# Stick-breaking attention: weights formed transposed in PSUM, queries and values over the full array

## The chip, the cores and the metric

The kernel runs on one core of one Trainium2 chip. The metric is the device time of one execution in microseconds (us); three runs of the kernel before gave 3334.37, 3337.85 and 3341.75, median 3337.85.

## What is computed

One decoder layer over 1024 tokens of width 1024, in float32. The part that matters here is the stick-breaking attention, 8 heads of width 64, computed for blocks of 128 tokens:

```python
z = jnp.einsum('bhtd,bhsd->bhts', q[:, :, t0:kl], k[:, :, :kl]).astype(jnp.float32) * scale
causal = s_idx < t_idx
log_beta = jax.nn.log_sigmoid(z)
log_one_minus = jnp.where(causal, jax.nn.log_sigmoid(-z), 0.0)
tail = lax.cumsum(log_one_minus, axis=3, reverse=True) - log_one_minus
w = jnp.where(causal, jnp.exp(log_beta + tail), 0.0)
outs.append(jnp.einsum('bhts,bhsd->bhtd', w.astype(v.dtype), v[:, :, :kl]))
```

Since log_sigmoid(z) = z - softplus(z) and log_sigmoid(-z) = -softplus(z), the weight is exp(z - R), where R is the sum of softplus(z) over the position itself and all later causal ones: a running sum taken from the right. Beside attention the layer has an mLSTM branch (4 heads), gates and projections, two layer norms, and PEER, which picks 128 of 16384 experts per token and sums their rows.

## The kernel before

**Blocks.** The tokens are cut into 8 token blocks of 128 and these into three groups (`BLOCKS`, line 66) of 2, 3 and 3, called block 0, 1 and 2 here. `main` (line 1141) takes each group through layer norm and projection, then attention merged with the mLSTM branch and the gates (line 1148), then the merge of branches, the keys and the choice of experts. Expert rows of five token blocks are gathered one by one: GpSimd issues an indirect DMA for a row of each of 128 tokens (line 1079) into one of K = 6 `vr` buffers, and VectorE multiplies and sums it (through `Chain`, line 139). These rows are sprinkled between the steps of the main chain by the times that the steps `yield`. The other three token blocks go through all 16384 experts as dense products at the end (`dense`, line 1009).

**Attention** (line 552) works through rows and chunks. A row is one head `e` of a pair `pr` and one token block `j`; it has `nb` key blocks, 1 to 8, and is cut into chunks of at most four: one chunk up to four key blocks, two beyond that. Blocks 0, 1 and 2 have 16, 24 and 24 rows, 16, 32 and 48 chunks, and 24, 96 and 168 key blocks. A chunk passes four steps, in a software pipeline (line 628) in which round k runs `s1(k)`, `s2(k-1)`, `s3(k-2)` and `s4(k-3)`:

- `s1` (line 575): TensorE multiplies the 64 rows of the head's queries with the keys (line 583, stationary operand 64 x 128) into a `z` bank and adds the causal mask (line 585). ScalarE forms softplus in `asp` (Abs, Exp, Ln) and its other part in `art` (Relu); three of the four passes scale by 0.125 or run in place.
- `s2` (line 594): VectorE takes the running sum from the right (line 597), carried from the row's first chunk to its second, and forms z * 0.125 minus it in `art` (line 599), reading z from PSUM; ScalarE takes the Exp.
- `s3` (line 602): TensorE transposes the weights, 128 columns at a time, into an `m` bank (line 607), and ScalarE copies them out to `awT` (line 609).
- `s4` (line 612): if all chunks of the row stand in `row["done"]`, TensorE multiplies values and weights (line 622, stationary operand 128 x 64) into an `m` bank, and ScalarE copies the 64 rows to `osT` (line 625).

**Order and buffers.** The code is traced and then scheduled: each engine's queue is in the order in which a planner's model finds instructions ready, with the code's order as priority, and each engine runs its queue strictly in that order. Tiles come from rings: `z` and `m` banks of PSUM, two each (line 181), `c2` tiles of 512 columns, seven (`NC2`, line 37), used by attention and by most other steps. A reader that is late keeps a slot, and what needs the slot waits. The descriptors of the indirect DMAs use a scratch of 8192 bytes per partition of SBUF (line 1228).

```python
        for k in range(N + 3):
            if k < N:
                s1(k)
            if 0 <= k - 1 < N:
                s2(k - 1)
            if 0 <= k - 2 < N:
                s3(k - 2)
            if 0 <= k - 3 < N:
                s4(k - 3)
```

Of the kernel before, what the change touches and what calls it, by code (L numbers as in the profile page):

```python
# [10 lines left out]
F32 = mybir.dt.float32  # L11
# [3 lines left out]
AF = mybir.ActivationFunctionType  # L15
OP = mybir.AluOpType
# [4 lines left out]
P = 128  # L21
# [12 lines left out]
ORDER = [(0, 1), (2, 3, 4)]  # L34
NC4 = 4
NR4 = 2
NC2 = 7
NCS = 7
RANKS = [(0, 0, 1, 16), (16, 1, 2, 8), (24, 2, 3, 5), (29, 3, 4, 4), (33, 4, 5, 3), (36, 5, 8, 2), (42, 8, 16, 1)]
NC50 = 50  # L40
# [79 lines left out]
def body(ctx: ExitStack, tc: tile.TileContext, a, out):  # L120
    nc = tc.nc
# [3 lines left out]
    vec, pe, pool, dma = nc.vector, nc.tensor, nc.gpsimd, nc.sync  # L125
# [49 lines left out]
    act = Act()  # L175

    def T(shape, dt, tag, bufs=1):
        return sb.tile(shape, dt, name=tag, tag=tag, bufs=bufs)

    def PT(tag, shape=(P, 512)):  # L180
        return ps.tile(list(shape), F32, name=tag, tag=tag, bufs={"g": 4, "z": 2, "m": 2}[tag])

    def c6(name, shape=(P, 4, W), dt=F32):
        return sb.tile(list(shape), dt, name=name, tag="c6", bufs=8)

    def c4(name, shape=(P, D)):
        return sb.tile(list(shape), F32, name=name, tag="c4", bufs=NC4)
# [4 lines left out]
    def c2(name, shape=(P, 512), dt=F32):  # L192
        return sb.tile(list(shape), dt, name=name, tag="c2", bufs=NC2)

# [3 lines left out]
    first = [c4("xt") for _ in BLOCKS[0]]  # L198
# [4 lines left out]
    ident = T([P, P], F32, "ident")  # L203
    make_identity(nc, ident)
    identr = T([P, P], F32R, "identr")
    vec.tensor_copy(identr, ident)
    alf = T([P, P], F32, "alf")
    vec.tensor_scalar(alf, ident, ALPHA, None, op0=OP.mult)
    zero = c2("zero")
# [213 lines left out]
    def planned(name, order=None, fast=False):  # L423
        us = units(name)
        r = []
        for u in (range(len(us)) if order is None else order):
            stream.items += [(p, fast) for p in us[u]]
            r.append(us[u])
        return r

    for i, blk in enumerate(BLOCKS):
        q = {"main": planned("wmain", (1, 2, 0, 3, 4, 6, 5), i in FAST), "gate": [], "mix": []}
# [18 lines left out]
    for i, tbs in enumerate(BLOCKS):  # L451
        o = Blk()
# [99 lines left out]
    def attention(o):  # L552
        o.os = c6("osT")
        kl = o.t0 + o.w
        work = []
        for pr in range(4):
            for j in range(o.n):
                for e in range(2):
                    nb = o.tbs[j] + 1
                    cs = [(4, nb - 4), (0, 4)] if nb > 4 else [(0, nb)]  # L560
                    row = {"pr": pr, "j": j, "e": e, "nb": nb, "carry": 0.0, "done": [], "n": len(cs)}
                    work += [(row, lo, n, i == 0) for i, (lo, n) in enumerate(cs)]
        kv = {}

        def load(pr):
            kt = c4("kt")
            dma.dma_start(kt[:, :kl], kTd[pr, :, :kl])
            vt = c4("vt", (P, NTB, P))
            dma.dma_start(vt[:, :kl // P, :], vSd[pr, :, :kl // P, :])
            kv[pr] = kt, vt  # L570

        load(0)
        live = {}

        def s1(k):
            row, lo, n, first = work[k]
            pr, w = row["pr"], n * P
            if pr + 1 not in kv and pr < 3:
                load(pr + 1)
            rows = slice(row["e"] * 64, row["e"] * 64 + 64)  # L580
            tsl = slice(row["j"] * P, (row["j"] + 1) * P)
            pz = PT("z")
            pe.matmul(pz[:, :w], o.qT[rows, pr, tsl], kv[pr][0][rows, lo * P:lo * P + w], start=True, stop=True)  # L583
            if first:
                pe.matmul(pz[:, w - P:w], identr, maskz, start=False, stop=True, skip_group_check=True)
            sp = c2("asp")[:, :w]
            act.activation(sp, pz[:, :w], AF.Abs, scale=0.125)
            act.activation(sp, sp, AF.Exp, scale=-1.0)
            act.activation(sp, sp, AF.Ln, bias=1.0)
            rt = c2("art")[:, :w]  # L590
            act.activation(rt, pz[:, :w], AF.Relu, scale=0.125)
            live[k] = pz[:, :w], sp, rt

        def s2(k):
            row = work[k][0]
            pz, sp, rt = live[k]
            vec.tensor_tensor_scan(sp[:, ::-1], sp[:, ::-1], rt[:, ::-1], row["carry"], OP.add, OP.add)
            row["carry"] = sp[:, 0:1]
            vec.scalar_tensor_tensor(rt, pz, 0.125, sp, op0=OP.mult, op1=OP.subtract)
            act.activation(rt, rt, AF.Exp)  # L600

        def s3(k):
            row, lo, n, first = work[k]
            rt = live.pop(k)[2]
            pw = PT("m")
            for s in range(n):
                pe.transpose(pw[:, s * P:(s + 1) * P], rt[:, s * P:(s + 1) * P], ident)
            wT = c2("awT")
            act.copy(wT[:, :n * P], pw[:, :n * P])
            row["done"].append((lo, n, wT))  # L610

        def s4(k):
            row = work[k][0]
            if len(row["done"]) < row["n"]:
                return
            rows = slice(row["e"] * 64, row["e"] * 64 + 64)
            po = PT("m")
            i = 0
            vt = kv[row["pr"]][1]
            for lo, n, wT in row["done"]:  # L620
                for s in range(n):
                    pe.matmul(po[rows, :P], vt[:, lo + s, row["e"] * 64:(row["e"] + 1) * 64],  # L622
                              wT[:, s * P:(s + 1) * P], start=i == 0, stop=i == row["nb"] - 1)
                    i += 1
            act.copy(o.os[rows, row["pr"], row["j"] * P:(row["j"] + 1) * P], po[rows, :P])

        N = len(work)
        for k in range(N + 3):
            if k < N:
                s1(k)  # L630
            if 0 <= k - 1 < N:
                s2(k - 1)
            if 0 <= k - 2 < N:
                s3(k - 2)
            if 0 <= k - 3 < N:
                s4(k - 3)
            yield 3.0 * (work[min(k, N - 1)][2] * P + 100) / 612

    def mlstm(o):
# [599 lines left out]
```

## Time and profile before

| | us |
|---|---|
| median of three runs | 3337.85 (3334.37 to 3341.75) |
| the profiled execution | 3336.88 |
| its span, first to last instruction | 3335.1 |
| stage of the dense experts | from about 2095 to 3215 |
| attention of block 0, 1, 2 | about 61 to 116, 453 to 690, 1308 to 1650 |

The profile is of one execution. PE is TensorE's products, PEld its loads of the stationary operand (they can run under products), DVE is VectorE, ACT ScalarE, POOL GpSimd. A record is one instruction as the profiler saw it; a float32 product appears as two records, a transpose as one. Starts are microseconds from the start of the span. The duration of a PE record includes its way through the pipeline, so the pace of a stream is read from start to start, not from durations. PEclk is the clock that TensorE was granted, 1.00 being 2.4 GHz and 0.50 being 1.2 GHz. In waits, "PE z L583 <- DVE art L599" says that PE stood idle before the instruction of line 583 that writes `z`, until DVE's instruction of line 599 had ended.

### The profile page before, as it was taken

To read this page: it belongs to the slowest core of one execution; us is meant where nothing else is said; L and a number is where in the kernel's file an instruction comes from. 1 tells how busy PE (TensorE), PEld (TensorE's weight loads), DVE (VectorE), ACT (ScalarE), POOL (GpSimd) and SP (SyncE) were. 2 spreads that over 40 slices of the span, in tenths; PEclk is the share of its full clock that TensorE was granted. 3 is DMA by queue.
4 is the path that set the end of the run, shared out by engine and by line. 5 is a ranking of instruction groups with operands and counts; after the bars stand their busy time and mean duration, and the time that the engine had idled before them with its cause. 6 is when DMAs were issued, how large, how long until landed. Compare 5 with 4: busy or idle time off the path is not lost.

```text
span 3335.1 us, 38987 instructions
## 1 busy us (share of the span) xinstructions
PE 2974.0 (89%) x12105; PEld 1982.6 (59%) x12105; DVE 2668.9 (80%) x5661; ACT 1101.9 (33%) x2560; POOL 1562.8 (47%) x1313
## 2 busy tenths in 40 slices
PE   7997999969899837999898967899999999999990
PEld 6786654545464535556655545566666666666660
DVE  5635999788699999989887999967776777777788
ACT  4626234430611458556413145111111111111110
POOL 0000156557534553556665343644445555554565
PEclk9998998969999968999899989999999999999995
DMA  6444699989979989898799889999999999999997
GB/s 213 136 146 143 234 350 323 323 281 381 376 271 317 359 273 320 306 340 267 244 373 363 308 303 312 335 361 352 353 346 355 357 353 348 348 355 337 361 329 265
DMA packets 341825, 1035.22 MB, mean 310 GB/s; under 512 B 38512, under 2 KB 95216, under 8 KB 341616
## 3 DMA queue, kind: packets, MB, share of 16 engines
q0 software_dynamic: 184320, 671.17, 56.0%
q1 hardware_dynamic: 157296, 361.55, 30.3%
q8 instruction: 96, 1.57, 0.2%
q14 instruction: 113, 0.93, 0.1%
HBM read 991.17 MB, written 41.42 MB: 310 GB/s over the span
## 4 chain that ended last, share of the span: by engine, by line
PE 67%; DVE 16%; issue 8%; ACT 6%; DMA 2%; POOL 1%; SPq 0%; DVEq 0%; POOLq 0%; ACTq 0%
PE g L274 15%; PE g L1019 13%; PE z L1019 6%; PE m L278 5%; PE m L276 5%; PE m L277 5%; PE g L784 3%; DVE acc L139 3%; PE m L622 3%; ACT ohB L161 2%; PE z L583 2%; DVE vr L139 2%; PE g L276 2%; PE g L278 2%; PE g L277 2%
## 5 line engine op out<-in xcount | busy, mean ns | idle before, releaser
L1079 POOL DMA_INDIRECT vr<-in_u_dram,vidx x640 | 772.9, 1208 | 1013.1 <-DVE V L139 384.5
L1079 POOL DMA_INDIRECT vr<-in_v_dram,vidx x640 | 786.1, 1228 | 729.6 <-DVE acc L139 271.2
L139 DVE SCALAR_TENSOR_TENSOR acc<-vr,w,acc 128x1024 f32<-128x1024 f32 x640 | 817.9, 1278 | 43.6 <-DMA vr<-in_v_dram,vidx 34.4
L139 DVE SCALAR_TENSOR_TENSOR vr<-vr,h1r 128x1024 f32<-128x1024 f32 x640 | 780.0, 1219 | 55.8 <-DMA vr<-in_u_dram,vidx 40.9
L1019 PE MATMUL g<-wf,y 128*128 128x512 f32 x1024 | 462.8, 594 | 14.7 <-DVE y L1043 14.7
L161 ACT ACTIVATE hl<-wf 128x512 fp32r<-128x512 f32 x256 | 160.5, 628 | 765.7 <-PE m L278 599.5
L251 DVE TENSOR_TENSOR hl<-wf,hl 128x512 fp32r<-128x512 f32 x256 | 179.1, 701 | 292.8 <-PE m L277 244.7
L276 PE MATMUL m<-h1s,hl 128*128 128x384 f32 x1024 | 394.7, 385 | 3.5 <-ACT y L161 3.5
L278 PE MATMUL m<-h1s,hl 128*128 128x384 f32 x1024 | 347.8, 340 | 2.7 <-DVE hl L251 2.6
L274 PE MATMUL g<-hT,wf 128*128 128x384 f32 x1024 | 342.7, 489 | 5.8 <-DVE gs L851 3.2
L277 PE MATMUL m<-h1s,hl 128*128 128x384 f32 x1024 | 346.0, 338 | 0.0
L1019 PEld LDWEIGHTS g<-wf,y 128*128 128x128 f32 x1024 | 193.1, 190 | 201.9 <-issue 171.3
L274 PEld LDWEIGHTS g<-hT,wf 128*128 128x128 f32 x1024 | 191.7, 191 | 136.1 <-issue 7.7
L1019 PE MATMUL z<-wf,y 128*128 128x512 f32 x512 | 240.6, 592 | 0.0
L276 PEld LDWEIGHTS m<-h1s,hl 128*128 128x128 f32 x1024 | 194.1, 190 | 34.0 <-issue 29.4
L277 PEld LDWEIGHTS m<-h1s,hl 128*128 128x128 f32 x1024 | 194.1, 190 | 29.2 <-issue 29.2
L278 PEld LDWEIGHTS m<-h1s,hl 128*128 128x128 f32 x1024 | 193.8, 189 | 4.3 <-DVE hl L251 3.3
L987 PE MATMUL z<-ohA,ohB 128*128 128x128 f32 x768 | 137.9, 320 | 47.1 <-ACT ohB L161 18.7
L274 PE MATMUL g<-h1T,wf 128*128 128x384 f32 x512 | 173.1, 493 | 1.5 <-ACT h1T L161 1.4
L1019 PEld LDWEIGHTS z<-wf,y 128*128 128x128 f32 x512 | 97.3, 190 | 122.5 <-issue 122.2
L622 PE MATMUL m<-awT,vt 128*64 128x128 f32 x992 | 150.2, 303 | 18.6 <-ACT awT L173 10.4
L987 PEld LDWEIGHTS z<-ohA,ohB 128*128 128x128 f32 x768 | 112.1, 210 | 74.5 <-ACT ohB L161 53.1
(332 smaller groups left out, 4461.6 us busy)
## 6 DMA issues: line engine op xcount, KB each, us to landing
wf<-in_uE_dram SPq DMA_DIRECT2D x128, 512.0 KB
wf<-in_v_dram SPq DMA_DIRECT2D x128, 512.0 KB
wf<-in_wmain_dram SPq DMA_DIRECT2D x84, 512.0 KB
wf<-in_wgate_dram SPq DMA_DIRECT2D x48, 512.0 KB
wf<-in_wq_dram SPq DMA_DIRECT2D x48, 512.0 KB
Gd<-stage SPq DMA_DIRECT2D x48, 512.0 KB
gp<-Gd SPq DMA_DIRECT2D x32, 768.0 KB
wf<-in_wout_dram SPq DMA_DIRECT2D x24, 512.0 KB
```

The costliest lines, as they stand in the source:

```text
L139: x = getattr(vec, op)(*args, **kw)
L161: x = nc.scalar.activation(o, i, f, **kw)
L251: vec.tensor_tensor(lo, src, hi, op=OP.subtract)
L274: pe.matmul(o, l[0], r[0], start=first, stop=last)
L276: pe.matmul(o, l[0], r[0], start=first, stop=False)
L277: pe.matmul(o, l[0], r[1], start=False, stop=False)
L278: pe.matmul(o, l[1], r[0], start=False, stop=last)
L622: pe.matmul(po[rows, :P], vt[:, lo + s, row["e"] * 64:(row["e"] + 1) * 64], wT[:, s * P:(s + 1) * P], start=i == 0, stop=i == row["nb"] - 1)
L784: pe.matmul(acc, yT[k // 4][:, k % 4, n * P:(n + 1) * P], wo[u][k // 2][:, k % 2, :], start=k == 0, stop=k == 7)
L987: pe.matmul(pg[:, k], B[:, k], A[:, k], start=True, stop=True)
L1019: pe.matmul(acc[d][c], y[:, d * P:(d + 1) * P], wv[:, c * 512:(c + 1) * 512], start=e == 0, stop=e == P - 1)
L1079: pool.indirect_dma_start(out=vr, out_offset=None, in_=use[0], in_offset=bass.IndirectOffsetOnAxis(ap=idx[:, s:s + 1], axis=0))
```

## The change

The queries of a row are copied once per row, scaled by 0.125, into half of a 128-row buffer `qz` whose other half stays zero, so the score product runs over all 128 rows of a pair's keys. The scores are copied from the `z` bank to SBUF (`azs`); the subtraction on VectorE and the Exp behind it go. Instead TensorE transposes the scores into the `m` bank and adds the running sum, transposed and negated by a product with the negated identity, and the Exp is taken on the way out of the bank. The value product takes both heads' columns of the values (128 wide) and only the row's half of the output is copied. The round becomes `s4(k-2)`, `s1(k)`, `s2(k-1)`, `s3(k-1)`. The `c2` ring gets one slot more, and the scratch of the indirect DMAs shrinks to 2048 bytes.

```diff
--- before.py
+++ after.py
@@ -34,7 +34,7 @@
 ORDER = [(0, 1), (2, 3, 4)]
 NC4 = 4
 NR4 = 2
-NC2 = 7
+NC2 = 8
 NCS = 7
 RANKS = [(0, 0, 1, 16), (16, 1, 2, 8), (24, 2, 3, 5), (29, 3, 4, 4), (33, 4, 5, 3), (36, 5, 8, 2), (42, 8, 16, 1)]
 NC50 = 50
@@ -204,6 +204,11 @@
     make_identity(nc, ident)
     identr = T([P, P], F32R, "identr")
     vec.tensor_copy(identr, ident)
+    nident = T([P, P], F32, "nident")
+    vec.tensor_scalar(nident, ident, -1.0, None, op0=OP.mult)
+
+    qz = T([P, 2, 2, P], F32, "qz")
+    vec.memset(qz, 0.0)
     alf = T([P, P], F32, "alf")
     vec.tensor_scalar(alf, ident, ALPHA, None, op0=OP.mult)
     zero = c2("zero")
@@ -574,39 +579,44 @@
 
         def s1(k):
             row, lo, n, first = work[k]
-            pr, w = row["pr"], n * P
+            pr, j, e, w = row["pr"], row["j"], row["e"], n * P
             if pr + 1 not in kv and pr < 3:
                 load(pr + 1)
-            rows = slice(row["e"] * 64, row["e"] * 64 + 64)
-            tsl = slice(row["j"] * P, (row["j"] + 1) * P)
+            rows = slice(e * 64, e * 64 + 64)
+            q = row["q"] = qz[:, (pr * o.n + j) % 2, e, :]
+            if first:
+                act.activation(q[rows], o.qT[rows, pr, j * P:(j + 1) * P], AF.Copy, scale=0.125)
             pz = PT("z")
-            pe.matmul(pz[:, :w], o.qT[rows, pr, tsl], kv[pr][0][rows, lo * P:lo * P + w], start=True, stop=True)
+            pe.matmul(pz[:, :w], q, kv[pr][0][:, lo * P:lo * P + w], start=True, stop=True)
             if first:
                 pe.matmul(pz[:, w - P:w], identr, maskz, start=False, stop=True, skip_group_check=True)
+            zs = c2("azs")[:, :w]
+            act.copy(zs, pz[:, :w])
             sp = c2("asp")[:, :w]
-            act.activation(sp, pz[:, :w], AF.Abs, scale=0.125)
+            act.activation(sp, pz[:, :w], AF.Abs)
             act.activation(sp, sp, AF.Exp, scale=-1.0)
             act.activation(sp, sp, AF.Ln, bias=1.0)
             rt = c2("art")[:, :w]
-            act.activation(rt, pz[:, :w], AF.Relu, scale=0.125)
-            live[k] = pz[:, :w], sp, rt
+            act.activation(rt, pz[:, :w], AF.Relu)
+            live[k] = sp, rt, zs
 
         def s2(k):
             row = work[k][0]
-            pz, sp, rt = live[k]
+            sp, rt, _ = live[k]
             vec.tensor_tensor_scan(sp[:, ::-1], sp[:, ::-1], rt[:, ::-1], row["carry"], OP.add, OP.add)
             row["carry"] = sp[:, 0:1]
-            vec.scalar_tensor_tensor(rt, pz, 0.125, sp, op0=OP.mult, op1=OP.subtract)
-            act.activation(rt, rt, AF.Exp)
 
         def s3(k):
+
             row, lo, n, first = work[k]
-            rt = live.pop(k)[2]
+            sp, _, zs = live.pop(k)
             pw = PT("m")
             for s in range(n):
-                pe.transpose(pw[:, s * P:(s + 1) * P], rt[:, s * P:(s + 1) * P], ident)
+                c = slice(s * P, (s + 1) * P)
+                pe.transpose(pw[:, c], zs[:, c], ident)
+                pe.matmul(pw[:, c], sp[:, c], nident, start=False, stop=True, skip_group_check=True)
             wT = c2("awT")
-            act.copy(wT[:, :n * P], pw[:, :n * P])
+            act.activation(wT[:, :n * P], pw[:, :n * P], AF.Exp)
             row["done"].append((lo, n, wT))
 
         def s4(k):
@@ -619,21 +629,20 @@
             vt = kv[row["pr"]][1]
             for lo, n, wT in row["done"]:
                 for s in range(n):
-                    pe.matmul(po[rows, :P], vt[:, lo + s, row["e"] * 64:(row["e"] + 1) * 64],
-                              wT[:, s * P:(s + 1) * P], start=i == 0, stop=i == row["nb"] - 1)
+                    pe.matmul(po[:, :P], vt[:, lo + s, :], wT[:, s * P:(s + 1) * P],
+                              start=i == 0, stop=i == row["nb"] - 1)
                     i += 1
             act.copy(o.os[rows, row["pr"], row["j"] * P:(row["j"] + 1) * P], po[rows, :P])
 
         N = len(work)
-        for k in range(N + 3):
+        for k in range(N + 2):
+            if 0 <= k - 2 < N:
+                s4(k - 2)
             if k < N:
                 s1(k)
             if 0 <= k - 1 < N:
                 s2(k - 1)
-            if 0 <= k - 2 < N:
-                s3(k - 2)
-            if 0 <= k - 3 < N:
-                s4(k - 3)
+                s3(k - 1)
             yield 3.0 * (work[min(k, N - 1)][2] * P + 100) / 612
 
     def mlstm(o):
@@ -1225,7 +1234,7 @@
     import concourse.bacc as bacc
     from concourse.bass_utils import run_bass_kernel_spmd
 
-    nc = bacc.Bacc("TRN2", target_bir_lowering=False, num_devices=1, dynamic_dma_scratch_size=8192)
+    nc = bacc.Bacc("TRN2", target_bir_lowering=False, num_devices=1, dynamic_dma_scratch_size=2048)
     arrays, aps = {}, {}
     for name, v in layout({k: np.asarray(v) for k, v in inputs.items()}).items():
         v = np.ascontiguousarray(v)
```

## Rows read from the trace of the kernel before

**Rows 1.** The page's head: busy us, share of the span, instructions.

```profile
PE 2974.0 (89%) x12105; PEld 1982.6 (59%) x12105; DVE 2668.9 (80%) x5661; ACT 1101.9 (33%) x2560; POOL 1562.8 (47%) x1313
```

**Rows 2.** Stretches: length; busy PE, PEld, DVE, ACT, POOL; PEclk, DMA share, GB/s.

```profile
60.00:118.00 58.00, 53.40 (x327) 41.36 (x327) 33.46 (x73) 46.19 (x140) 0.00 (x0) 0.90 0.41 142
445.00:690.00 245.00, 234.70 (x865) 131.37 (x863) 205.25 (x359) 122.08 (x276) 135.53 (x115) 0.94 0.88 315
1300.00:1500.00 200.00, 187.97 (x745) 106.56 (x744) 175.78 (x250) 108.66 (x224) 110.40 (x95) 0.95 0.90 324
1500.00:1660.00 160.00, 141.29 (x716) 99.69 (x715) 143.32 (x222) 88.65 (x202) 99.23 (x74) 0.86 0.77 254
2095.00:3215.00 1120.00, 1119.93 (x4302) 770.94 (x4303) 813.66 (x1286) 197.43 (x361) 586.07 (x463) 1.00 0.97 352
3215.00:3336.00 121.00, 32.92 (x120) 21.08 (x118) 104.89 (x128) 2.63 (x5) 67.65 (x59) 0.64 0.77 276
```

**Rows 3.** Groups by line and shape: count, busy us, mean ns, idle.

```profile
L622 PE MATMUL m<-awT,vt 128*64 128x128 f32 x992 | 150.2, 303 | 18.6 <-ACT awT L173 10.4 <-DVE mkn L691 3.2 <-ACT cqk L161 2.3
L607 PE MATMUL m<-ident,art 128*128 128x128 f32 x288 | 56.2, 308 | 4.9 <-ACT art L161 2.4 <-ACT awT L173 0.8 <-ACT mnd L161 0.7
L173 ACT ACTIVATE osT<-m 64x128 f32<-64x128 f32 x96 | 25.9, 270 | 66.2 <-PE m L622 61.9 <-issue 3.1 <-ACT art L161 0.3
```

**Rows 4.** Chain of waits, 1409 to 1420 and dense: start, length.

```profile
1409.28 1.02 PE m L622 x8
1410.30 0.37 PE m L607 x2
1410.67 1.05 PE z L583 x2
1411.72 7.92 PE g L274 x18
1419.64 1.46 PE m L622 x12
...
2102.78 3.43 PE g L1019 x8
```

**Rows 5.** Timeline of PE around line 825: start us, us, what.

```profile
922.46 0.83 PE L825 MATMUL m<-k,pq 128*128 128x128 f32 x6
923.13 2.10 PE L274 MATMUL g<-h1T,wf 128*128 128x384 f32 x6
```

**Rows 6.** Timeline of PE around four transposes (line 394).

```profile
906.76 0.60 PE L394 MATMUL m<-ident,xt 128*128 128x128 f32 x4
907.20 0.81 PE L274 MATMUL g<-h1T,wf 128*128 128x384 f32 x2
```

**Rows 7.** Waits of PE, whole span: us in total, times, longest.

```profile
PE z L583 <- DVE art L599: 10.2, 9, 2.6
...
PE m L607 <- ACT art L161: 2.4, 3, 2.1
```

**Rows 8.** Line 599 alone by stretch: length, DVE busy, PEclk, DMA share.

```profile
60.00:118.00 58.00, 5.62 (x16) 0.90 0.41 142
445.00:690.00 245.00, 17.65 (x32) 0.94 0.88 315
1300.00:1500.00 200.00, 15.99 (x27) 0.95 0.90 324
1500.00:1660.00 160.00, 13.51 (x22) 0.86 0.77 254
```

**Rows 9.** Groups by line and shape, 512 columns: count | busy us, mean ns.

```profile
L597 DVE TENSOR_TENSOR_SCAN asp<-asp,art 128x512 f32<-128x512 f32 x48 | 60.5, 1261 | 32.1 <-ACT asp L161 15.3 <-ACT art L161 13.0 <-issue 3.3
...
L161 ACT ACTIVATE art<-art 128x512 f32<-128x512 f32 x48 | 30.1, 627 | 21.1 <-DVE art L599 20.8
L161 ACT ACTIVATE asp<-z 128x512 f32<-128x512 f32 x48 | 28.5, 594 | 23.1 <-PE z L583 10.7 <-PE z L585 5.2 <-DVE asp L597 2.0
```

**Rows 10.** DMA queues on the page: packets, MB, share of 16 engines' span.

```profile
q0 software_dynamic: 184320, 671.17, 56.0%
```

## The prediction, made before the changed kernel was built or run

> **What bounds the kernel now.** I read the page's head first: PE is busy 2974.0 us of the span of 3335.1, DVE 2668.9 [rows 1]. That is a mean over stages with different limits, so next comes the table of stretches [rows 2]; the reader should compare, in each, the PE and DVE busy time with the length. From 2095 to 3215 the dense experts run with PE busy 1119.93 of 1120 us, and after it 121 us of expert rows are left on DVE. Neither holds a line of this change, and nothing there starts earlier than the main chain allows, so what is gained before 2095 should arrive whole at the end. Attention lies in three stretches, one for each block of rows: 60 to 118, 445 to 690 and 1300 to 1660. In 445 to 690 PE is busy 234.70 of 245 us and DVE 205.25; in 1300 to 1500, 187.97 of 200 and 175.78; in 1500 to 1660 the two are level, 141.29 and 143.32 of 160. PE is first, DVE close behind. ACT (122.08 of 245) has room. So the change is worth what it takes from PE, provided DVE loses as much.
>
> **What PE does twice.** The value product (line 622) has 992 records and the copy of its result to osT 96 [rows 3]. Eight heads times 36 key blocks are 288 products, and an fp32 product leaves two records (the score stands as x2 in [rows 4]): 576. There are 64 rows (8 heads, 8 token blocks), so 64 copies. The surplus is 416 records and 32 copies. The code says why: in one round of the loop `s3(k-2)` runs ahead of `s4(k-3)`, so for a row of two chunks `done` is already full when `s4` comes for the first chunk, and the whole row is multiplied; a round later it is multiplied again. Rows of two chunks are those of 5 to 8 blocks: 8 x 26 = 208 products, 416 records. In the new loop `s4(k-2)` stands ahead of `s3(k-1)`: at the first chunk `done` lacks the second, `s4` returns, and the repeat is gone, though the diff does not speak of it.
>
> **What the 64-wide products cost.** The chain of waits gives PE's pace [rows 4]. Eight 512-column records of the dense stage take 3.43 us, 0.429 each. A score pair on 64 rows of the array takes 1.05, so 0.19 over 2 x 0.429. A value group of 8 records takes 1.02 and one of 12 takes 1.46: 0.11 a record, and 0.14 over. A stretch of 18 projection records between two 64-wide groups takes 7.92 against 7.72: 0.20 over. That is 0.53 a chunk; where no projection stands between, less, and I take 0.5. Products of 128 x 128 show no such step: six records of line 825 take 0.67 us to the next product's start [rows 5], 0.112 each, and four transposes take 0.44 to the start of the projection behind them [rows 6].
>
> **The sum on PE**, in order: block 0 (16 chunks, 24 key blocks), block 1 (32, 96), block 2 (48, 168).
> - Added: one 128 x 128 fp32 product with the negated identity per key block, two records at 0.112 = 0.223 us: +5.4, +21.4, +37.5.
> - Repeats removed (0, 40, 168 products at 2 x 0.11): 0, -8.8, -37.0.
> - Scores and values over the full array, 0.5 a chunk: -8, -16, -24. The number of columns is the same, so the streaming time stays.
> - The score waited for the z bank until DVE had done line 599: 10.2 us in 9 waits [rows 7]. In the new kernel only ACT reads z, so -10.2, which I give to blocks 1 and 2 by halves.
> - Together -2.6, -8.5, -28.6 = -39.7 us.
>
> The transposes (288) move from the weights to the scaled scores and keep their price. No row shows a transpose and an accumulating product alternating in one bank, 576 switches. Bounds: nothing, or a saving if it fills gaps, by [rows 6], where transposes and fp32 products follow each other without a step; 0.14 each by the 64-wide groups, 81 us. I take nothing, since the shapes are those of [rows 6].
>
> **DVE.** The subtraction of line 599 goes: 5.62, 17.65, and 15.99 + 13.51 = 29.5 us by block [rows 8]. In blocks 1 and 2 this is more than PE's gain, so DVE does not become the bound in its place; nearly equal in block 2, which is why I count no gain beyond PE's. The two set-up operations (`nident`, the `qz` memset) lie at the start, where DVE waits for x; without that cover they cost about 1 us, by the subtraction of 512 columns.
>
> **ACT.** Per chunk a copy out of z is added (0.594 us for 512 columns, as the Abs beside it), the Exp from SBUF (0.627) goes [rows 9], and an Exp takes the place of the copy out of the m bank, one pass over the same bank. Level. Per row there is a copy of q on 64 partitions, 64 of 0.27 us as osT's [rows 3], against 32 repeats dropped: +8.6 us in all, 4.3 of them in block 0, where ACT has 46.19 of 58. Hidden under PE; without that cover 4 us.
>
> **Buffers.** A chunk now takes four c2 tiles instead of three, from 8 slots instead of 7: 2.0 chunks in flight instead of 2.3. One chunk of 512 columns needs five passes of ACT at 0.6, the scan at 1.261 [rows 9], some 2.5 us of PE and one more pass, under 8 us; with two in flight 4 us a chunk, and block 2 has 360/48 = 7.5. I cost it at nothing; if only one fits it is the rival of the scan, made worse.
>
> **The gather's scratch** shrinks to a quarter. The 1280 gathers make 184320 packets [rows 10], 144 each, 9 on each of 16 DMA engines; K = 6 buffers allow at most six in flight, 54 an engine. No row says when the scratch is full: between nothing and a stall of all expert rows. I take nothing, as the buffers, not the scratch, limit the flight now. The Trainium skill ("DMA: Bandwidth & Descriptors", Terms) gives 16 bytes a descriptor: by that an estimated 128 fit in 2048 bytes, more than 54, and the sum is the same.
>
> **The sum:** 3336.9 us is the profiled execution (the span and 1.8 us around it), 1.0 under the median of 3337.85. 3336.9 - 39.7 + 1.0 = **3298 us**. Expert rows keep their order among the main chain's steps, so the tail after 3215 stays.
>
> **Rivals.**
> 1. *The clock rises too.* PEclk is 0.94, 0.95 and 0.86 in the three long stretches [rows 2]: 29, 20 and 45 us at the lower of the two levels, 1.2 GHz. A us there does half the work, so at most 47 us come back. The part of the z waits that starts such a stretch is gone, and PE has more full-array work. Against: DVE is at 143.32 of 160 where most of it lies, so half at best: 3298 - 23 = 3275.
> 2. *The expert rows pace these stretches.* DMA share is 0.88 and 0.90 [rows 2], DVE 0.84 and 0.88; if rows are late anyway, PE only waits more, and all is absorbed: 3336. Against: 0.97 is reached in the dense stage, so the DMA has room for 7 to 9%, and the change asks for 3 to 8%.
> 3. *A wait on the scan (slower).* PE now takes the scan's result itself, one round after the score; before, transposes came two rounds later, behind an Exp. In PE's queue the projections stand behind it; in DVE's an expert row of 1.2 us can stand ahead of the scan. PE's direct waits on DVE cost 10.2/9 = 1.1 us each [rows 7]. At each of the 80 chunks of blocks 1 and 2 that is 88: 3386. It decides from 0.5 us a chunk (39.7/80). Against: waits for the old Exp were 2.4 us in all [rows 7], because the order on PE follows modelled readiness: values stand ahead of transposes in [rows 4]'s stretch though the code has them behind.
> 4. *Weight loads no longer hide.* A 64-row pair pays for its load ([rows 4], 0.19). If full-array products did so too, 1152 records would cost about 0.1 more: 3298 + 115 = 3413. The Trainium skill ("TensorE: Matmul & The Clock Gate", Part 3) says that a load overlaps running products only when the row group differs, which would give this. The trace disagrees: 0.112 a record [rows 5].
> 5. *The repeat stays*, should `done` fill earlier than I read: 3298 + 46 = 3344.
>
> **Chances.** Forecast 0.56, rival 1 0.18, rival 2 0.10, rival 3 0.12, rivals 4 and 5 with the scratch 0.04. About 0.2% (6.7 us) is what a measurement can tell from no change. Faster: 0.56 + 0.18 = 0.74; same: 0.10; slower: 0.12 + 0.04 = 0.16. The range goes from rival 1 with a little more of the clock (3262) to rivals 2 and 5 (3345); it leaves out rival 3 at its full price, rival 4, and the upper end of the switches.
>
> **What would show it.** Right: 576 records of the value product and 576 with the identity, near 0.11 us apart; 64 osT copies; no waits of the score on DVE; DVE's busy time 53 us lower; the dense stage starting some 40 us earlier, three quarters of that between 1300 and 1660. Wrong: PE waiting on the scan for over 40 us in total, steps between transposes and products, ACT waiting on c2 slots that hold PE up, or gather times on POOL that grow.

## The result, and the profile after

The changed kernel takes 3288.74 us (median of four runs, 3285.06 to 3292.95) against 3336.11 for the kernel before beside it: a ratio of 0.9856, 95% interval 0.9838 to 0.9873. The forecast was 3298, in a range of 3262 to 3345. The profiled execution took 3287.69 us, its span 3285.6.

The head of the changed kernel's page, as in [rows 1]:

```profile
PE 2934.3 (89%) x12265; PEld 2013.0 (61%) x12265; DVE 2626.9 (80%) x5567; ACT 1095.3 (33%) x2590; POOL 1581.4 (48%) x1313
```

PE is 39.7 us less busy, DVE 42.0. (The forecast's 39.7 was of time, not of busy time.) Next, groups by line and shape of the changed kernel (count | busy us, mean ns | idle before), as in [rows 3]:

```profile
L617 PE MATMUL m<-nident,asp 128*128 128x128 f32 x576 | 113.8, 298 | 17.8 <-DVE asp L606 17.6
...
L632 PE MATMUL m<-awT,vt 128*128 128x128 f32 x576 | 87.4, 293 | 11.3 <-ACT awT L161 10.8 <-DVE mnd L717 0.3
...
L632 PEld LDWEIGHTS m<-awT,vt 128*128 128x128 f32 x576 | 77.6, 202 | 30.8 <-ACT awT L161 19.3 <-issue 4.5 <-DVE mnd L717 1.0
...
L173 ACT ACTIVATE osT<-m 64x128 f32<-64x128 f32 x64 | 17.3, 270 | 77.4 <-PE m L632 74.7 <-issue 2.2
```

The value product has 576 records in place of 992 and there are 64 copies to `osT` in place of 96: the repeat is gone. The product with the negated identity adds 576 records. Its mean of 298 ns is the way through the pipeline; the pace stands in the chain of waits, in the stretch that answers to [rows 4] (start us, length us, what):

```profile
1402.46 7.78 PE g L279 x18
1410.24 0.89 PE m L632 x8
1411.13 0.11 PE m L616
1411.24 0.22 PE m L617 x2
...
1412.13 0.86 PE z L590 x2
```

Eight value records take 0.89 where they took 1.02, the stretch of 18 projection records between them 7.78 where it took 7.92, a score pair 0.86 where it took 1.05; a transpose takes 0.11 and the two records of an identity product 0.22, and the two kinds alternate without a step. In this stretch every price of the sum on PE is met. What PE waits for (us in total, times, longest), to be held against [rows 7]:

```profile
PE m L617 <- DVE asp L606: 17.6, 12, 4.5
PE g L1028 <- DVE y L1052: 16.6, 3, 14.2
...
PE m L632 <- ACT awT L161: 10.8, 20, 0.7
...
PE z L590 <- ACT art L161: 3.6, 5, 1.2
```

The score no longer waits for DVE. The scan has become a wait of 17.6 us in 12 places. (The 14.2 us that the dense stage waits for `y` come up again below.)

Now the stages. From here on, a stage of attention runs from the first score of its block to the first product of the output projection, the dense stage from DVE's first weighting of `y` to its last, and the tail from there to the end of the span. Stretches of the kernel before, in the order attention of block 1, of block 2, dense stage, tail (length; busy PE, PEld, DVE, ACT, POOL; PEclk, DMA share, GB/s):

```profile
451.90:824.50 372.60, 336.59 (x1212) 199.44 (x1212) 317.71 (x549) 141.96 (x324) 229.66 (x189) 0.89 0.90 325
1306.80:1726.20 419.40, 395.26 (x1669) 245.61 (x1670) 367.23 (x543) 203.82 (x437) 250.51 (x202) 0.93 0.87 308
2037.50:3239.20 1201.70, 1182.15 (x4547) 816.04 (x4548) 887.47 (x1523) 213.05 (x389) 627.36 (x495) 0.99 0.96 348
3239.20:3335.10 95.90, 8.72 (x21) 3.58 (x19) 84.14 (x107) 0.00 (x0) 50.85 (x45) 0.56 0.76 278
```

The same stages of the changed kernel:

```profile
452.70:821.60 368.90, 330.94 (x1325) 218.31 (x1324) 318.05 (x532) 140.72 (x336) 251.25 (x200) 0.90 0.93 344
1298.20:1685.70 387.50, 364.60 (x1670) 251.32 (x1671) 341.88 (x499) 194.58 (x433) 258.63 (x200) 0.95 0.90 330
1994.30:3196.80 1202.50, 1180.39 (x4547) 814.55 (x4548) 888.05 (x1522) 213.15 (x389) 623.75 (x496) 0.99 0.96 347
3196.80:3285.60 88.80, 8.53 (x20) 3.42 (x18) 78.97 (x103) 0.00 (x0) 45.84 (x41) 0.58 0.75 278
```

The dense stage ends 42.4 us sooner (3239.2 to 3196.8), 31.9 of it from the attention of block 2 (419.4 to 387.5), and the tail is 7.1 us shorter. What the tail holds is shown by the groups of DVE in it, of the kernel before and then of the changed one:

```profile
L139 DVE SCALAR_TENSOR_TENSOR acc<-vr,w,acc 128x1024 f32<-128x1024 f32 x49 | 62.9, 1284 | 6.9 <-DMA vr<-in_v_dram,vidx 5.6
```

```profile
L139 DVE SCALAR_TENSOR_TENSOR acc<-vr,w,acc 128x1024 f32<-128x1024 f32 x45 | 57.8, 1284 | 5.9 <-DMA vr<-in_v_dram,vidx 4.6
```

49 and 45 expert rows of the last token block are left behind the dense stage. That the tail depends on them is what the experiments test.

### The profile page after: what moved, and what is told of

It is laid out like the page before. It is cut to its first block, busy times and chain, and to the rows that moved or that the text cites. A ratio compares the mean times of both kernels' runs of the same rounds, so it can differ in the third digit from the quotient of the medians.

```text
span 3285.6 us, 39190 instructions
## 1 busy us (share of the span) xinstructions
PE 2934.3 (89%) x12265; PEld 2013.0 (61%) x12265; DVE 2626.9 (80%) x5567; ACT 1095.3 (33%) x2590; POOL 1581.4 (48%) x1313
## 4 chain that ended last, share of the span: by engine, by line
PE 66%; DVE 15%; issue 7%; ACT 7%; DMA 3%; POOL 1%; SPq 0%; DVEq 0%; ACTq 0%; POOLq 0%
PE g L279 15%; PE g L1028 13%; PE z L1028 6%; PE m L283 5%; PE m L281 5%; PE m L282 5%; PE g L793 3%; DVE acc L139 3%; ACT ohB L161 2%; PE g L283 2%; PE g L281 2%; PE g L282 2%; PE m L617 2%; DVE vr L139 2%; PE z L590 1%
## 5 line engine op out<-in xcount | busy, mean ns | idle before, releaser
L1088 POOL DMA_INDIRECT vr<-in_u_dram,vidx x640 | 784.3, 1226 | 968.3 <-DVE V L139 385.7
L1088 POOL DMA_INDIRECT vr<-in_v_dram,vidx x640 | 793.4, 1240 | 706.9 <-DVE acc L139 297.6
L256 DVE TENSOR_TENSOR wf<-wf 128x1024 fp32r<-128x1024 f32 x68 | 83.1, 1222 | 68.9 <-ACT wf L161 66.8
```

Source lines behind the costliest of these rows:

```text
L256: vec.tensor_tensor(lo, src, hi, op=OP.subtract)
L1088: pool.indirect_dma_start(out=vr, out_offset=None, in_=use[0], in_offset=bass.IndirectOffsetOnAxis(ap=idx[:, s:s + 1], axis=0))
```

## The experiments

Milestones of all kernels, worked out from their traces (us; time is the median, ratio with its interval against the kernel before run beside it; att. 1 and att. 2 are the lengths of the attentions of blocks 1 and 2; rows are expert rows in DVE's queue). The kernel before was run anew beside each set of kernels, so two kernels are compared by their ratios; 0.001 is 3.3 us. The stages are of one execution each: the kernel before and e5, or the changed kernel, e10 and e11, which have the same attention, differ by up to 5 us in a stage.

```
kernel          time     ratio [95%]             att. 1  att. 2  rows in  dense    rows  tail
                                                                 att.1+2  ends     left
before          3336.11  -                       372.7   419.5   389      3239.2   49     95.9
after           3288.74  0.9856 [0.9838,0.9873]  368.9   387.4   397      3196.8   45     88.8
e1_no_repeat    3330.70  0.9978 [0.9966,0.9990]  368.2   414.3   387      3220.1   54    104.4
e2_full_array   3297.55  0.9878 [0.9861,0.9894]  365.3   409.0   405      3213.2   40     82.1
e3_both         3298.63  0.9881 [0.9864,0.9898]  355.1   392.6   381      3191.5   55    105.0
e4_after_sub    3301.97  0.9891 [0.9875,0.9908]  369.7   392.4   390      3208.5   44     87.4
e7_no_product   3272.68  0.9804 [0.9787,0.9820]  327.7   354.3   352      3120.7   83    145.0
e8_two_products 3288.86  0.9846 [0.9830,0.9862]  385.2   409.1   426      3217.4   33     71.2
e9_after_repeat 3293.66  0.9857 [0.9841,0.9874]  382.2   415.8   424      3222.5   34     72.7
e10_rate        3289.19  0.9845 [0.9829,0.9862]  368.3   389.3   395      3201.2   45     88.1
e5_scratch      3336.85  0.9992 [0.9980,1.0003]  372.8   424.2   390      3241.4   49     96.4
e6_after_nc7    3288.29  0.9850 [0.9832,0.9867]  375.3   383.3   400      3201.9   42     84.5
e11_fewer_rows  3227.97  0.9665 [0.9648,0.9682]  368.6   389.5   398      3196.8    0     27.9
e12_k7          3309.43  0.9906 [0.9888,0.9923]  378.7   384.8   405      3246.4   32     68.5
```

The first four take the change apart: the theory was that the terms on PE add up at the end, the rival that DVE's load sets what they are worth.

**The repeat alone removed (e1)** (kernel before, two calls swapped):

```diff
-            if 0 <= k - 2 < N:
-                s3(k - 2)
             if 0 <= k - 3 < N:
                 s4(k - 3)
+            if 0 <= k - 2 < N:
+                s3(k - 2)
```

> The kernel before with s4(k-3) ahead of s3(k-2) in the round: value products and osT copies once per row (576 records, 64 copies), all else as before. By PE's sum: 0, -8.8 and -37.0 us by block, so 3290 us against 3336, with most of it between 1300 and 1726. If DVE is the bound in block 2 (143.32 of 160 us busy in its second half), PE only waits more and at most half comes: 3315 or above.

Measured 0.9978, some 7 us, where the sum had 46. Attention of block 2, then the tail:

```profile
1294.70:1709.00 414.30, 380.19 (x1334) 221.96 (x1335) 364.06 (x539) 194.77 (x413) 256.52 (x200) 0.86 0.87 309
...
3220.10:3324.50 104.40, 9.48 (x23) 3.87 (x21) 90.50 (x112) 0.00 (x0) 57.23 (x50) 0.56 0.78 282
```

Block 2 runs 335 fewer records (1334 for 1669), 37 us at 0.11, and is 5.1 us shorter. The granted clock is 0.86 where it was 0.93 (and 0.91 in e5, the kernel before but for its scratch): by (1 - PEclk) x 2 x length, 116 us at 1.2 GHz instead of 59 to 76, of which half is lost, 20 to 29 us by this estimate. The mean over the whole run fell too, in every run: 0.926 to 0.931 in seven, against 0.934 to 0.939 in ten of the kernel before. PE idles 34 us of it instead of 24, beside a DVE that is busy 364 of 414; in the whole span the score waits for line 599 longer than the 10.2 us of [rows 7]:

```profile
PE z L583 <- DVE art L599: 26.6, 13, 4.5
```

The dense stage ends 19 us sooner and the tail returns 8.5, with 54 rows left.

**Scores and values over the full array, alone (e2)** (kernel before, repeat and subtraction kept, scratch 2048 to make room):

```diff
+    qz = T([P, 2, 2, P], F32, "qz")
+    vec.memset(qz, 0.0)
...
-            pe.matmul(pz[:, :w], o.qT[rows, pr, tsl], kv[pr][0][rows, lo * P:lo * P + w], start=True, stop=True)
+            q = qz[:, (pr * o.n + row["j"]) % 2, row["e"], :]
+            if first:
+                act.activation(q[rows], o.qT[rows, pr, tsl], AF.Copy)
+            pe.matmul(pz[:, :w], q, kv[pr][0][:, lo * P:lo * P + w], start=True, stop=True)
...
-                    pe.matmul(po[rows, :P], vt[:, lo + s, row["e"] * 64:(row["e"] + 1) * 64],
-                              wT[:, s * P:(s + 1) * P], start=i == 0, stop=i == row["nb"] - 1)
+                    pe.matmul(po[:, :P], vt[:, lo + s, :], wT[:, s * P:(s + 1) * P],
+                              start=i == 0, stop=i == row["nb"] - 1)
```

> The kernel before with queries zero-padded to 128 rows and 128-wide values, scratch 2048; repeats, subtraction and Exp stay. By PE's sum the steps around 64-wide products go, 0.5 us a chunk: -8, -16, -24, so 3288 us. If DVE paces blocks 1 and 2: 3315 or above. If only idle PE time is filled: 3330 to 3336.

Measured 0.9878, 41 us of the 48 costed: of all parts the one that pays. But it does not pay where it was costed. The dense stage ends 26.0 us sooner, and 9 rows fewer are left, which shortens the tail by 13.8. Attention of block 2, with 24 us costed, is 10.5 us shorter while it holds 9 rows more:

```profile
1294.20:1703.20 409.00, 368.32 (x1669) 250.41 (x1670) 381.14 (x583) 207.78 (x457) 264.20 (x208) 0.96 0.90 324
```

Scores and values were not taken apart, so which of the two pays is not known.

**Both together (e3)** (the two edits above):

> Both at once: repeats dropped, full array, but no product with the identity, and the subtraction stays on DVE with its hold on the z bank. By PE's sum alone -45.8 - 48 = -94 us: 3242. If DVE, with 205 of 245, 170 of 193 and 143 of 160 us busy, is next after PE, the two gains do not add: DVE's idle time of blocks 1 and 2 is 40 + 23 + 17 us, of which half at best can go: 3290 to 3300, no better than the changed kernel (3289).

Measured 0.9881, no better than the full array alone. The end of the dense stage moves 48 us from the kernel before's, 22 more than with the full array alone, and the tail is 23 longer (55 rows left for 40). With the repeats 405 rows stand in the two attentions, without them 381: what their absence takes from the main chain comes back as rows in the tail.

**The subtraction put back into the changed kernel (e4)**, its result unused, so that nobody waits for it:

```diff
             row["carry"] = sp[:, 0:1]
+            vec.tensor_tensor(rt, live[k][2], sp, op=OP.subtract)
```

> The changed kernel with a subtraction of the same size put back on DVE behind the scan (scores less running sums in SBUF, result unused), 96 of them, about 53 us of DVE. If PE's queue sets these stretches, it costs little: 3289 to 3300. If the gain came from DVE, it takes most of it back: 3320 to 3336.

Measured 0.9891 against 0.9856, about 12 us, between the two expectations. No wait of PE carries it; the dense stage just ends 11.7 us later (3208.5; 3201.2 and 3201.9 in e10 and e6, which do no more on DVE than the changed kernel). The rows left are 44, nearly as many as without it (45). The prediction let DVE's 53 us count for nothing.

So the terms on PE do not add up at the end. The next four ask why, by moving PE's work in the changed kernel both ways; the theory now was that the rows, a second stream of fixed size, set the end.

**The identity product left out (e7)** (the weights are then not those of the reference, as the expectation says):

```diff
-                pe.matmul(pw[:, c], sp[:, c], nident, start=False, stop=True, skip_group_check=True)
...
-            act.activation(wT[:, :n * P], pw[:, :n * P], AF.Exp)
+            act.activation(wT[:, :n * P], pw[:, :n * P], AF.Exp, scale=2.0 ** -10)
```

> The changed kernel without the product with the identity: the running sum is left out of the weights, and the Exp scales by 2**-10 so that values stay finite. The scan still runs for the carry. By PE's sum 64 us of products and 18 us of waits on the scan go: 3210 to 3230 against 3289. If the clock gives products back (fewer of them, more time at 1.2 GHz, as when the repeats were dropped alone), 3270 to 3289.

Measured 0.9804, 17 us under the changed kernel, where PE's sum has 64 and the scan's waits 18. The sum is right for the main chain: the dense stage ends at 3120.7, 76 us sooner. Dense stage, tail, and DVE's first group in the tail:

```profile
1918.10:3120.70 1202.60, 1179.49 (x4545) 814.85 (x4546) 887.76 (x1522) 212.75 (x389) 615.97 (x495) 0.99 0.96 347
3120.70:3265.70 145.00, 9.44 (x22) 3.83 (x21) 127.78 (x141) 0.00 (x0) 90.63 (x79) 0.54 0.84 306
```

```profile
L139 DVE SCALAR_TENSOR_TENSOR acc<-vr,w,acc 128x1024 f32<-128x1024 f32 x83 | 106.7, 1285 | 13.2 <-DMA vr<-in_v_dram,vidx 11.1
```

83 rows are left instead of 45, the tail grows from 88.8 to 145.0 us, and 56 of the 76 us are handed back.

**The identity product twice, at half size (e8)**:

```diff
-    vec.tensor_scalar(nident, ident, -1.0, None, op0=OP.mult)
+    vec.tensor_scalar(nident, ident, -0.5, None, op0=OP.mult)
...
+                pe.matmul(pw[:, c], sp[:, c], nident, start=False, stop=True, skip_group_check=True)
```

> The changed kernel with the product with the negated identity done twice at half size (same result): 288 more fp32 products. By PE's sum +64 us: 3353. If PE has slack that the clock fills: 3289 to 3315, with less time at 1.2 GHz between 1298 and 1686.

64 us of added work on PE cost nothing: 3288.86. Attention of block 2, dense stage, tail:

```profile
1322.80:1731.90 409.10, 392.67 (x2005) 280.86 (x2006) 361.13 (x546) 200.74 (x437) 278.76 (x213) 0.98 0.92 333
2039.50:3217.40 1177.90, 1177.84 (x4548) 814.75 (x4549) 861.13 (x1472) 212.88 (x390) 600.94 (x484) 1.00 0.96 348
3217.40:3288.60 71.20, 8.27 (x20) 3.38 (x18) 63.52 (x91) 0.00 (x0) 32.86 (x29) 0.59 0.70 256
```

The two attentions grow by 38 of the 64 us (table). Three things pay. The clock in block 2 is 0.98 instead of 0.95, though it is 0.97 in e4 and e6 as well, which leave PE's work as it was. In the attention of blocks 1 and 2 run 426 rows instead of 397, 33 are left, and the tail is 17.6 us shorter. And the dense stage is 24.6 us shorter, PE busy 1177.84 of 1177.90: the wait of line 1028 for `y`, 14.2 us at the longest in the changed kernel, is absent. In the changed kernel that wait ends 58.6 us into the dense stage, and up to there DVE has rows of the token block before among the choice of the last experts. These are DVE's rows in the first 58.6 us, of the changed kernel and then of this one:

```profile
L139 DVE SCALAR_TENSOR_TENSOR acc<-vr,w,acc 128x1024 f32<-128x1024 f32 x18 | 22.9, 1272 | 0.0
```

```profile
L139 DVE SCALAR_TENSOR_TENSOR vr<-vr,h1r 128x1024 f32<-128x1024 f32 x9 | 10.8, 1204 | 0.0
```

Here the rows of the block before had all run, and the first of the 9 starts 32 us into the stage; e9, which does not wait either, has 8, the first after 37 us. So this part as well seems to go back to rows that ran earlier; it is read from the two orders, and no run tests it alone.

**The repeat put back into the changed kernel (e9)**:

```diff
-            po = PT("m")
...
+            for _ in range(row["n"]):
+                po = PT("m")
```

> The changed kernel with the repeat put back: rows of two chunks are multiplied with the values twice, at the end of the row, 208 products and 32 copies more. By PE's sum +46 us: 3335. If products are nearly free beside DVE, as dropping the repeats alone said (-7): 3289 to 3305.

0.9857 against 0.9856: 46 us of work on PE cost nothing that can be told. The dense stage ends 25.7 us later and the tail is 16.1 shorter in the profiled execution, the longest of the four.

**A faster pace for the main chain in the dense stage (e10)** (changed kernel):

```diff
-RATES = {"mix": 1.0, "branch": 1.0, "keys": 1.0, "choose": 1.0, "last": 1.0, "dense": 1.0}
+RATES = {"mix": 1.0, "branch": 1.0, "keys": 1.0, "choose": 1.0, "last": 1.0, "dense": 1.05}
```

> The changed kernel with the dense stage's steps rated 5% longer, so that more expert rows are placed among them: some 25 of the 45 rows left behind the dense stage move into it. The tails of five kernels so far give 1.55 us a row: 3250 if the DMA engines (share 0.97 in that stage) take the rows beside the weights; 3285 to 3295 if the dense stage grows by what the tail loses.

3289.19, and 45 rows are left as before: the lever does not reach them, so this run says nothing of what fewer rows would bring.

The last four. Two test parts that were costed at nothing, one the theory directly, one a use of it.

**Rows left out (e11)** (the last 45 of the last token block's second pass):

```diff
-            for s in range(P):
+            for s in range(P - 45 if tb == 6 else P):
```

> The changed kernel without the last 45 expert rows of the last token block's second pass (their gathers and their multiply-adds are left out, so that block's rows of the output lack 45 of 128 terms). In the changed kernel 45 rows stand behind the last dense product, and the tail from there to the end is 88.8 us. Theory (the end is set by the rows left behind the dense stage, the dense stage itself ends where TensorE's sum puts it): the dense stage ends at 3197 plus or minus 6, none or few rows are left, the tail falls to 22 to 35 us, and the time to 3222 to 3240 us. Rival A (rows do not set the end; DMA, GpSimd or the layer norm of the last block does): 3275 to 3292 us. Rival B (the 45 rows save time where they are spread, not at the end: the rows before them move up and the dense stage ends sooner too): below 3215 us.

3227.97, in the theory's range and outside the rivals'. Attention of block 2, dense stage, tail:

```profile
1296.80:1686.20 389.40, 364.81 (x1669) 251.10 (x1670) 343.12 (x499) 194.71 (x433) 259.70 (x201) 0.95 0.91 331
1994.80:3196.80 1202.00, 1179.67 (x4546) 814.12 (x4547) 887.58 (x1523) 213.04 (x389) 617.31 (x491) 0.99 0.96 347
3196.80:3224.70 27.90, 9.14 (x22) 3.77 (x20) 22.80 (x58) 0.00 (x0) 0.00 (x0) 0.75 0.19 75
```

The dense stage ends at 3196.8 as in the changed kernel, and the whole 60.9 us between the two spans come off the tail. With 27.9 at no row, 88.8 at 45 and 145.0 at 83, a row left behind costs (88.8 - 27.9) / 45 = 1.35 to (145.0 - 27.9) / 83 = 1.41 us; over the whole table it is 1.27 to 1.42.

**Scratch of 2048 bytes alone (e5)** (kernel before):

```diff
-    nc = bacc.Bacc("TRN2", target_bir_lowering=False, num_devices=1, dynamic_dma_scratch_size=8192)
+    nc = bacc.Bacc("TRN2", target_bir_lowering=False, num_devices=1, dynamic_dma_scratch_size=2048)
```

> The kernel before with only the scratch space of the dynamic DMA descriptors cut from 8192 to 2048 bytes. Theory (this part of the change costs nothing, as the prediction took it): 3333 to 3341 us, ratio 0.998 to 1.002, and the gathers on POOL keep their 1208 and 1228 ns. Rival (the smaller ring makes POOL wait for landed descriptors): the gathers' mean on POOL rises, more than 49 expert rows are left behind the dense stage, and the time goes over 3345 us.

0.9992: nothing. The gathers on POOL, by count | busy, mean ns:

```profile
L1079 POOL DMA_INDIRECT vr<-in_v_dram,vidx x640 | 791.1, 1236 | 728.5 <-DVE acc L139 287.7 <-issue 78.9 <-DVE y L1043 70.7
L1079 POOL DMA_INDIRECT vr<-in_u_dram,vidx x640 | 767.7, 1200 | 1016.8 <-DVE V L139 383.9 <-DVE vr L139 321.7 <-issue 86.8
```

**Seven shared buffers in the changed kernel (e6)**:

```diff
-NC2 = 8
+NC2 = 7
```

> The changed kernel with 7 of the shared 2 KB buffers in place of 8. The prediction costed the buffers at nothing with 8 slots for the same four tiles per chunk. Theory (the eighth slot is slack): 3283 to 3295 us, and the score products wait for their PSUM bank no longer than the 3.6 us (the wait on ACT's Relu) that the changed kernel shows. Rival (with fewer slots ACT's copy of the scores waits for a buffer to come free, and the bank is held with it): the attention of block 2 grows from 387 to over 395 us and the time to over 3300.

3288.29, block 2 at 383.3: the eighth slot is slack, as costed. The score's waits for ACT to leave its bank came to 4.6 and 0.9 us, over the 3.6 expected, at no cost that shows.

**A seventh buffer for the rows (e12)** (`K = 7`, paid for as the expectation says):

```diff
-K = 6
+K = 7
-NC2 = 8
+NC2 = 7
...
-            act.copy(zs, pz[:, :w])
+            act.activation(zs, pz[:, :w], AF.Copy, scale=-1.0)
...
-                pe.matmul(pw[:, c], sp[:, c], nident, start=False, stop=True, skip_group_check=True)
+                pe.matmul(pw[:, c], sp[:, c], ident, start=False, stop=True, skip_group_check=True)
...
-            act.activation(wT[:, :n * P], pw[:, :n * P], AF.Exp)
+            act.activation(wT[:, :n * P], pw[:, :n * P], AF.Exp, scale=-1.0)
```

> The changed kernel with a seventh buffer for the gathered expert rows and the streamed weights (K = 7), for which the eighth shared buffer is given up and the negated identity goes: the scores are copied with scale -1 and the exponential is taken with scale -1, so that the plain identity serves. The same results are computed. Theory (the rows that are left behind the dense stage set the end, and they pass through it at 2.4 us each because a row's buffer comes free late): the dense stage takes in more than its 496 rows, fewer than 45 are left, and the time is 3225 to 3280 us. Rival (the order of VectorE's queue, written ahead of the run, sets how many rows stand behind the last dense product, whatever the buffers): 40 to 50 rows are left and the time is 3280 to 3296 us.

Neither: 3309.43, a ratio of 0.9906 against 0.9856, so 17 us slower than the changed kernel. The dense stage takes 495 rows, as the changed kernel's takes 496, which speaks against buffers that held it back; 32 are left, since 8 rows more stand in the two attentions and 4 more between them. In the profiled execution, the longest of the four, the loss lies between the attentions of blocks 1 and 2: 516.6 us where the changed kernel takes 476.7, and most of it at the start. The first stretch and the rest, here and then in the changed kernel:

```profile
830.70:880.00 49.30, 34.04 (x105) 17.54 (x103) 48.07 (x59) 6.33 (x21) 38.33 (x37) 0.88 1.02 408
880.00:1347.30 467.30, 357.75 (x1384) 226.26 (x1383) 394.46 (x1201) 212.62 (x613) 194.37 (x165) 0.89 0.82 291
```

```profile
821.60:870.00 48.40, 48.40 (x161) 25.14 (x159) 39.17 (x48) 18.57 (x55) 33.13 (x31) 1.00 0.98 374
870.00:1298.20 428.20, 336.48 (x1327) 215.14 (x1326) 397.00 (x1205) 199.68 (x579) 196.81 (x165) 0.91 0.87 314
```

In the output projection PE runs 105 records in 49 us where it ran 161 in 48, and DVE then stands 64.4 us for one result (9.8 in the changed kernel):

```profile
DVE V L811 <- ACT sc L161: 64.4, 1, 64.4
```

PE's own waits there are of no engine: from 863 to 899 its records come one by one, put down to "issue", which means that it waited for nothing that the profile shows:

```profile
PE g L744 <- issue: 18.6, 8, 3.2
...
PE m L397 <- issue: 10.4, 6, 3.1
```

None of the other thirteen traces has such a wait of PE of over 0.9 us. The DMA share around it is 1.02, but the changed kernel's is 0.98 with no such wait, so the cause stays open. (The seventh buffer is shared by the rows and the split activations of line 301, not by the weights as the expectation has it.) No version that beats the changed kernel was found.

## Why the prediction was right, and which step failed

**Size and direction** came out: 39.7 us were forecast and 42.4 arrived at the end of the dense stage. By block the forecast was -2.6, -8.5 and -28.6; attention of block 0 took 0.5 more (168.2 to 168.7), block 1 3.8 less with another 5.5 in the stretch behind it, block 2 31.9 less. The rest of what arrived is the tail, 7.1 us, for which the forecast had nothing. (The prediction drew the line at 3215 and read the 121 us behind it as rows alone; dense products run until 3239, so the tail before was 95.9.)

**The prices** held. Records at 0.11, score pairs and steps of the 64-wide products, no step between transposes and products, the repeat, the scratch (e5), the buffers (e6): each as the rows of the trace before said. Two signs that the prediction named came otherwise. DVE's busy time fell by 42.0 us and not 53: the 96 records of line 599 last 53 us in all, but each overlaps its neighbours by some 0.1 us (the subtraction of e4 adds 40.7); and the gathers' mean time on POOL rose from 1208 and 1228 ns to 1226 and 1240, which was to count as a sign of wrong but is 1.5% at most. Rival 4 is out: eight value records take 0.89 us while their weight loads take 202 ns each. The Trainium skill ("TensorE: Matmul & The Clock Gate", Part 3) says in its list of what overlaps that a load does so only where the row group differs, and just before also where it goes to the background weight buffer. The trace disagrees with the first again, with 0.111 us a record; no run here shows which buffer a load goes to.

**The step that failed** is in the part on what bounds the kernel: "what is gained before 2095 should arrive whole at the end", with its companion in the sum, "the tail after 3215 stays". The end is set by two streams, the main chain and the rows left behind it at some 1.4 us each (e11). In e7 the main chain moves by about PE's sum (76 of 82 us), and 45 rows fewer stand in the two attentions; in e1 nearly as many rows stay there as before (387 and 389), and the chain moves by 19 of 46. There are 1280 rows in all, and what stands in no stage ahead is left for the tail. Measured at the end, the terms are: full array 41 of 48 (e2), repeats 7 (e1) or none (e3 against e2, e9) of 46, the identity product 17 (e7) or none (e8) of 64, the subtraction 12 of none (e4). They do not add up, since what each is worth differs with the kernel that it is taken from. So the total was met in part by luck: two large terms of opposite sign, 46 and 64, both count for little, and the full array alone gives 41 of the 47 us measured.

**Why this change kept its gain** when e7 gave most of its back is read from the rows: although attention of block 2 is 32 us shorter it takes in 199 rows (201 before), block 1 takes 198 (188), and 45 are left rather than 49. Time taken from DVE is only a part of it. Busy DVE in block 2 fell from 367.23 to 341.88 us; the prediction wrote that DVE "does not become the bound in its place" and gave the freed 53 us no worth, and e4 gives them 12. But e4, with that time back on DVE, still leaves 44 rows, and e2, which takes nothing from DVE, leaves 40. Where a row stands is written into DVE's queue ahead of the run, by the planner's model ("Order and buffers" above). Why that model puts 352 rows into the two attentions in e7, 397 in the changed kernel and 405 in e2 is not shown: no run changes the order alone.

**Rivals.** Rival 1 came in part: PEclk in block 2 rose from 0.93 (0.91 in e5) to 0.95 (the same in e10 and e11), by the formula above 20 to 38 us less at 1.2 GHz, an estimated 10 to 19 us of time, so the other terms gave some 22 (18 against e5) of the 28.6 forecast there. Rival 2 was named for the stretches of attention; its place is the tail. Rival 3 came as 17.6 us in 12 places, not 80, under the 40 that were to count as wrong. Rival 5 did not come, and e9 shows that it would have cost about nothing and not 46. The forecast let the clock stand still. Removed repeats lowered it in block 2 (0.93 to 0.86 in e1, 0.96 in e2 to 0.91 in e3), while the removed identity product left it at 0.96 (e7), and e2, where PE idles 41 us of block 2 against 34 in e1, has 0.96 as well. The 0.98 of e8 is hardly above the 0.97 of e4 and e6. Why the removed repeats lowered it and the removed product did not stays open.

## What to carry to other kernels

A sum on the busiest engine says when the main chain ends, not when the kernel ends: look for a second stream that is fitted in between, count what is left of it behind the last stage and price one piece, before calling a gain whole. Work taken off the busiest engine was partly returned wherever fewer pieces of the second stream then stood in the shortened stage (e3, e7), and kept where no fewer did (e2, the change itself); so count the pieces in each stage, before and after. Take a change apart on the chip even when the total is met, since here two of its terms were worth little and one costed at nothing was not.

## What was not expected of the hardware

- Removing the repeats lowered TensorE's granted clock: 335 fewer records in block 2 took it from 0.93 (0.91 in e5) to 0.86 (e1), and from 0.96 (e2) to 0.91 (e3), so that part of what the sum took away came back at 1.2 GHz. This is no rule: in e7, 337 fewer left it at 0.96 where the changed kernel has 0.95.
- Half of the array costs more than the whole: a score on 64 rows took 1.05 us a pair and one on 128 rows 0.86, eight values on 64 columns 1.02 and on 128 columns 0.89, for the same number of streamed columns.
- With one more buffer for the rows (e12) PE stood 29 us of a stretch of 36 for nothing that the profile shows, and the kernel was 17 us slower; the cause is open.
